# Transposes of probabilities, queries and keys by transposing DMAs, and scores in four PSUM banks, in a two-layer hybrid decoder step

## The chip, the cores and the metric

The kernel runs as one program on one core of a Trainium2 chip. The metric is the time of one execution in device microseconds. Each run executes the whole program once; the times below are of separate runs. The engines are called PE (TensorE matmul), PEld (TensorE weight load), DVE (VectorE), ACT (ScalarE), POOL (GpSimd) and SP (SyncE, which issues all DMAs of this kernel). "Window" means 256 of the 4096 prompt tokens; there are 16 of them.

## The reference

The step has two layers on 4096 prompt tokens and 8 x 4 sample tokens. Layer 0 is a scan plus gated linear attention; the change does not touch it. Layer 1 is sliding-window attention: 16 query heads of 64 on 2 key heads, each block of 128 queries sees its own and the previous block of 128 keys, and a learned sink logit joins the denominator.

```python
def sink_attention(q, k, v, q_pos, k_pos, sinks):
    s = jnp.einsum('...qhgd,...khd->...hgqk', q, k) * (SWA_HEAD_DIM ** -0.5)
    ...
    s = jnp.where(allowed[..., None, None, :, :], s, -jnp.inf)
    sink = sinks.astype(jnp.float32).reshape(SWA_KV_HEADS, SWA_GROUP, 1, 1)
    m = jnp.maximum(jnp.max(s, axis=-1, keepdims=True), sink)
    pr = jnp.exp(s - m)
    denom = jnp.sum(pr, axis=-1, keepdims=True) + jnp.exp(sink - m)
    return jnp.einsum('...hgqk,...khd->...qhgd', pr / denom, v)
...
    q = rope(rms_norm(q.reshape(n, l, SWA_HEADS, SWA_HEAD_DIM), p['q_norm_g']), pos)
    k = rope(rms_norm(k.reshape(n, l, SWA_KV_HEADS, SWA_HEAD_DIM), p['k_norm_g']), pos)
...
    return x + o.astype(x.dtype) @ p['w_out'], ...
```

## The kernel before

The program has three phases; the change lies in `phase2`, layer 1, which takes roughly the last 1400 us. Every float32 matrix product is made of three float16 products (high x high, high x low, low x high), so weights, activations, probabilities, queries and keys exist as pairs of float16 tiles.

For each window, `instream` projects the tokens to q, k, v (`mmA`, lines 334 to 336) and to the gate (`mmB`, lines 325 to 327). `heads` norms and rotates a block of 128 tokens and leaves its high and low halves in `s16`, with tokens in the partitions. `turn` (lines 1565 to 1572) brings the 64-wide heads into the partitions: eight TensorE transposes of 128 x 128 for each half of the queries, four for the keys, into a PSUM tile `pt`, which ACT copies to `qT` or `kT`. For one window that is 2 blocks x (8 + 8 + 4) = 40 transposes.

`attn` goes through 8 units for a window: 2 blocks x 2 groups of 4 heads x 2 key heads. For a unit, `scores` (line 1692) puts 16 matmuls of 128 columns into one PSUM tile of two banks, copies the previous block's half on ACT (line 1703), lays the masked half over it on DVE (line 1706), runs `softmax` (DVE and ACT in turn) and splits the probabilities on ACT (`Ph`, line 1710) and POOL (`Pl`, line 1711). Two units later `turnP` (line 1714) turns both with eight TensorE transposes, ACT copies the result to `PT` (line 1720), and DVE multiplies it by the mask to `PC` (line 1722). `values` then runs the 12 matmuls of two units with `PT` and `PC` (line 1760), and gates the result to `og`. `out` multiplies the `og` of the window before with the output weights (lines 325 to 327), adds the residual (line 1804) and stores it (line 1805).

`merge` interleaves these generators by the costs that they yield and by the weights E1 (attention), E2 (output) and so on. The instructions recorded so are then put in a final order for each engine by the framework's scheduler, which works with estimated times; the engines run that order strictly and meet at semaphores. All DMAs are issued by SP, in one order, and an SP instruction that waits holds all that stand behind it.

The lines that matter for the turns:

```python
                nc.tensor.transpose(pt[:, a, i], s[:, i], self.ident16)
        PT = P.tile([128, 8, 128], F16, name="PT", bufs=2)
        nc.scalar.activation(PT, pt.rearrange("p a i n -> p (a i) n"), AF.Copy, bias=0.0, scale=1.0)
```

Of the kernel before, what the change touches and what calls it, by code (L numbers as in the profile page):

```python
# [36 lines left out]
E1, E2, E3 = 120.0, 70.0, 30.0  # L37
# [69 lines left out]
class K:  # L107
# [1332 lines left out]
    def phase2(self, es1, tail):  # L1440
# [34 lines left out]
        psc = self.pool("p2sc", bufs=1, es=el, space=PSUM)  # L1475
        ppt = self.pool("p2pt", bufs=1, es=el, space=PSUM)
        pmm = self.pmm
        ptt = Rota(self.pta, self.ptb)
        psc = self.pool("p2sc", bufs=1, es=el, space=PSUM)
# [41 lines left out]
        n = NW  # L1521
# [8 lines left out]
        def instream(w):  # L1530
# [22 lines left out]
            for b, t in blocks:  # L1553
# [11 lines left out]
                def turn(i, s16, qT=qT, kT=kT):  # L1565
                    pt = ptt.tile([128, 8, 128], F16, name="pt")
                    for a in range(8 if i < 2 else 4):
                        nc.tensor.transpose(pt[:, a], s16[:, a], self.ident16)  # L1568
                    if i < 2:
                        nc.scalar.activation(qT[:, 8 * i:8 * i + 8], pt, AF.Copy, bias=0.0, scale=1.0)  # L1570
                    else:
                        nc.scalar.activation(kT.rearrange("p a b n -> p (a b) n"), pt[:, 0:4], AF.Copy, bias=0.0, scale=1.0)
# [119 lines left out]
        def scores(W, b, prev, g, kv, out):  # L1692

            ps = psc.tile([128, 4, 2, 128], F32, name="ps")
            for i in range(4):
                q = W["q"][b][:, 2 * (4 * g + i) + kv]
                for a, k in enumerate((prev[0] if prev else None, W["k"][b])):
                    if k is not None:
                        nc.tensor.matmul(ps[:, i, a], q, k[:, kv, 0], start=True, stop=False)  # L1699
                        nc.tensor.matmul(ps[:, i, a], q, k[:, kv, 1], start=False, stop=True)  # L1700
            Sc = P.tile([128, 4, 128], F32, name="Sc", bufs=2)
            if prev:
                nc.scalar.activation(Sc, ps[:, :, 0], AF.Copy, bias=0.0, scale=1.0)
            else:
                nc.gpsimd.memset(Sc, -1e30)
            nc.vector.copy_predicated(Sc, mkc.bitcast(I32)[:, None, :].to_broadcast([128, 4, 128]), ps[:, :, 1])
# [27 lines left out]
        def attn(W, Wp):  # L1734
# [40 lines left out]
            for u in range(11):  # L1775
# [10 lines left out]
                if 2 <= u < 10:  # L1786
                    unit, p = pend.pop(0)
                    pend2.append((unit, turnP(*p)))
                if u < 8:
                    next(sc)  # L1790
                yield 2.8
# [358 lines left out]
```

## Time and profile before

| | us |
|---|---|
| median of 3 runs | 3290.13 |
| lowest and highest | 3287.15, 3292.01 |
| the profiled execution's own time | 3289.11 |
| its span in the trace | 3287.3 |
| PE busy | 3150.1 (96%) |
| DVE, ACT, POOL busy | 2054.4 (62%), 1688.5 (51%), 1261.2 (38%) |

The profile is one execution, taken by the hardware's profiler. A row of instructions gives how long one took and what ended the idle time before it; matmuls overlap each other, so the distance from one to the next, and not the duration of one, is what PE pays for it. The chain is the work that ended last, followed back from the end of the span or of a stretch. The time outside the span is 1.8 us.

### The profile page before, as it was taken

To read this page: it belongs to the slowest core of one execution; us is meant where nothing else is said; L and a number is where in the kernel's file an instruction comes from. 1 tells how busy PE (TensorE), PEld (TensorE's weight loads), DVE (VectorE), ACT (ScalarE), POOL (GpSimd) and SP (SyncE) were. 2 spreads that over 40 slices of the span, in tenths; PEclk is the share of its full clock that TensorE was granted. 3 is DMA by queue.
4 is the path that set the end of the run, shared out by engine and by line. 5 is a ranking of instruction groups with operands and counts; after the bars stand their busy time and mean duration, and the time that the engine had idled before them with its cause. 6 is when DMAs were issued, how large, how long until landed. Compare 5 with 4: busy or idle time off the path is not lost.

```text
span 3287.3 us, 68398 instructions
## 1 busy us (share of the span) xinstructions
PE 3150.1 (96%) x27293; PEld 2458.2 (75%) x27293; DVE 2054.4 (62%) x4785; ACT 1688.5 (51%) x4054; POOL 1261.2 (38%) x1292
## 2 busy tenths in 40 slices
PE   6898879899999999999999999999999999999999
PEld 5687766687788777788877667777777777777777
DVE  8869998644444443444446477666666666666675
ACT  4386556233344343343345366565555656555664
POOL 7824241211111211111111565554555555555552
PEclk9799989999999999999999999999999999999999
DMA  4297467411111112211113212111111111101111
GB/s 128 60 252 176 95 149 223 121 46 49 46 49 46 44 45 71 58 50 46 43 53 122 72 36 62 41 40 41 36 42 40 34 37 37 34 28 41 40 32 43
DMA packets 329521, 222.79 MB, mean 68 GB/s; under 512 B 142544, under 2 KB 302240, under 8 KB 329056
## 3 DMA queue, kind: packets, MB, share of 16 engines
q1 hardware_dynamic: 329200, 218.41, 24.2%
q8 instruction: 214, 3.51, 0.4%
q14 instruction: 107, 0.88, 0.1%
HBM read 164.94 MB, written 53.23 MB: 66 GB/s over the span
## 4 chain that ended last, share of the span: by engine, by line
PE 75%; DVE 11%; ACT 4%; issue 4%; DMA 4%; POOL 3%; SPq 1%; DVEq 0%; POOLq 0%; ACTq 0%
PE mm L325 13%; PE mm L326 13%; PE mm L327 13%; PE mm L334 7%; PE mm L335 7%; PE mm L336 7%; PE po L1760 3%; PE pt L1718 2%; PE ps L1699 2%; PE ps L1700 2%; PE pt L1568 1%; DVE z L777 1%; POOL xl L314 1%; DVE x L312 1%; DMA wst<-in_w_in 1%
## 5 line engine op out<-in xcount | busy, mean ns | idle before, releaser
L325 PE MATMUL mm<-ogh,woh 128*128 128x256 f16 x1472 | 401.3, 273 | 1.4 <-DVE xr L1346 1.4
L326 PE MATMUL mm<-ogl,woh 128*128 128x256 f16 x1472 | 401.3, 273 | 0.5 <-POOL ogl L1772 0.5
L327 PE MATMUL mm<-ogh,wol 128*128 128x256 f16 x1472 | 401.3, 273 | 0.0
L314 POOL TENSOR_TENSOR xl<-x,xh 128x512 f16<-128x512 f32 (+1 forms) x196 | 261.3, 1355 | 319.1 <-ACT xh L313 306.1
L1683 ACT ACTIVATE Sc<-Sc,ng,rq 128x128 f32<-128x128 f32 x512 | 245.6, 482 | 107.1 <-DVE ng L1677 105.7
L272 POOL TENSOR_TENSOR acc<-acc,sq 128x512 f32<-128x512 f32 x48 | 61.8, 1288 | 565.4 <-issue 370.4
L1711 POOL TENSOR_TENSOR Pl<-Sc,Ph 128x512 f16<-128x512 f32 x128 | 153.3, 1198 | 275.6 <-ACT Ph L1710 244.9
L326 PEld LDWEIGHTS <-woh 128*128 128x128 f16 x2112 | 207.2, 98 | 36.4 <-issue 9.8
L325 PEld LDWEIGHTS <-woh 128*128 128x128 f16 x2112 | 207.2, 98 | 31.6 <-issue 4.6
L336 PEld LDWEIGHTS <-xl 128*128 128x128 f16 x1536 | 151.0, 98 | 106.0 <-issue 6.7
L334 PEld LDWEIGHTS <-xh 128*128 128x128 f16 x1536 | 150.9, 98 | 102.5 <-issue 17.7
L327 PEld LDWEIGHTS <-wol 128*128 128x128 f16 x2112 | 207.1, 98 | 25.5 <-issue 3.1
L335 PEld LDWEIGHTS <-xh 128*128 128x128 f16 x1536 | 151.0, 98 | 84.0 <-issue 5.1
L325 PE MATMUL mm<-xh,wuh 128*128 128x256 f16 (+1 forms) x544 | 151.6, 283 | 14.2 <-ACT us L727 6.9
L313 ACT ACTIVATE xh<-x 128x512 f16<-128x512 f32 (+1 forms) x196 | 117.8, 618 | 75.6 <-DVE x L312 61.7
L326 PE MATMUL mm<-xl,wuh 128*128 128x256 f16 (+1 forms) x544 | 151.4, 284 | 4.9 <-POOL xl L314 4.9
L1720 ACT ACTIVATE PT<-pt 128x1024 f16<-128x1024 f16 x128 | 129.6, 1013 | 42.1 <-PE pt L1718 42.1
L327 PE MATMUL mm<-xh,wul 128*128 128x256 f16 (+1 forms) x544 | 151.1, 283 | 0.0
L312 DVE TENSOR_TENSOR x<-x,rb 128x512 f32<-128x512 f32 (+1 forms) x188 | 136.5, 781 | 22.5 <-ACT rb L302 18.2
L1346 DVE SCALAR_TENSOR_TENSOR xr<-mm,soa,xr 128x512 f32<-128x512 f32 x64 | 47.7, 745 | 160.5 <-PE mm L327 155.8
L326 PE MATMUL mm<-xl,wi1gah 128*128 128x256 f16 x512 | 141.4, 277 | 3.0 <-POOL xl L314 3.0
L327 PE MATMUL mm<-xh,wi1gal 128*128 128x256 f16 x512 | 141.0, 276 | 2.4 <-DVE wi1gal L245 2.4
(730 smaller groups left out, 10558.9 us busy)
## 6 DMA issues: line engine op xcount, KB each, us to landing
x<-in_xT SPq DMA_DIRECT2D x128, 256.0 KB
wst<-in_w_in SPq DMA_DIRECT2D x64, 256.0 KB
xr<-in_xT SPq DMA_DIRECT2D x64, 256.0 KB
h_d<-xr SPq DMA_DIRECT2D x64, 256.0 KB
x<-h_d SPq DMA_DIRECT2D x64, 256.0 KB
xr<-h_d SPq DMA_DIRECT2D x64, 256.0 KB
out_yT<-xr SPq DMA_DIRECT2D x64, 256.0 KB
wst<-in_w_out SPq DMA_DIRECT2D x48, 256.0 KB
```

Source lines behind the costliest of these rows:

```text
L312: nc.vector.tensor_mul(x, x, rb[:, None, :].to_broadcast([128, 2, n]))
L313: nc.scalar.activation(h, x, AF.Copy, bias=0.0, scale=1.0)
L314: nc.gpsimd.tensor_sub(l, x, h)
L325: nc.tensor.matmul(ps, wh[:, k0 + k, c], xh[k], start=(k == 0), stop=False)
L326: nc.tensor.matmul(ps, wh[:, k0 + k, c], xl[k], start=False, stop=False)
L327: nc.tensor.matmul(ps, wl[:, k0 + k, c], xh[k], start=False, stop=(k == n - 1))
L334: nc.tensor.matmul(ps, xh[k][:, t], wh[:, k, c0:c1], start=(k == 0), stop=False)
L335: nc.tensor.matmul(ps, xh[k][:, t], wl[:, k, c0:c1], start=False, stop=False)
L336: nc.tensor.matmul(ps, xl[k][:, t], wh[:, k, c0:c1], start=False, stop=(k == n - 1))
L1683: nc.scalar.activation(Sc[:, i], Sc[:, i], AF.Exp, bias=ng[:, i:i + 1], scale=scale[:, i:i + 1], accum_out=de[:, i:i + 1])
L1711: nc.gpsimd.tensor_sub(Pl, Sc, Ph)
L1720: nc.scalar.activation(PT, pt.rearrange("p a i n -> p (a i) n"), AF.Copy, bias=0.0, scale=1.0)
```

## The change

The transposes of `turn` and `turnP` leave TensorE, PSUM and ACT: SP issues a transposing DMA from `s16` to `qT` or `kT`, and from `Pp` (the high and low probabilities, now one tile) to `PT`. The latter is issued as soon as the softmax has ended, into three `PT` buffers where there were two. The multiplication by the mask stays on DVE, in `masked`, called later than `turnP` was. The scores of a unit go in two halves of one bank each, and four banks rotate: two of their own and two that the turns used. The copy on ACT and the masked copy on DVE are made for each half. E2 goes from 70 to 90, and the loop over the units has 10 steps in place of 11.

```diff
-E1, E2, E3 = 120.0, 70.0, 30.0
+E1, E2, E3 = 120.0, 90.0, 30.0
...
-        psc = self.pool("p2sc", bufs=1, es=el, space=PSUM)
+        psc = Rota(self.pool("p2sa", bufs=1, es=el, space=PSUM), self.pool("p2sb", bufs=1, es=el, space=PSUM), self.pta, self.ptb)
...
                 def turn(i, s16, qT=qT, kT=kT):
-                    pt = ptt.tile([128, 8, 128], F16, name="pt")
-                    for a in range(8 if i < 2 else 4):
-                        nc.tensor.transpose(pt[:, a], s16[:, a], self.ident16)
                     if i < 2:
-                        nc.scalar.activation(qT[:, 8 * i:8 * i + 8], pt, AF.Copy, bias=0.0, scale=1.0)
+                        nc.sync.dma_start_transpose(qT[:, 8 * i:8 * i + 8], s16.rearrange("p a n -> p (a n)"))
...
-            ps = psc.tile([128, 4, 2, 128], F32, name="ps")
-            for i in range(4):
...
+            for j in range(2):
+                ps = psc.tile([128, 2, 2, 128], F32, name="pt")
+                for i in range(2):
...
+                So = Sc[:, 2 * j:2 * j + 2]
+                if prev:
+                    nc.scalar.activation(So, ps[:, :, 0], AF.Copy, bias=0.0, scale=1.0)
+                nc.vector.copy_predicated(So, mkc.bitcast(I32)[:, None, :].to_broadcast([128, 2, 128]), ps[:, :, 1])
             yield from softmax(Sc, snk[:, kv, 4 * g:4 * g + 4], W["rq"][b][:, g].rearrange("p (i k) -> p k i", k=2)[:, kv], 2.0**14, P)
-            Ph = P.tile([128, 4, 128], F16, name="Ph", bufs=3)
-            Pl = P.tile([128, 4, 128], F16, name="Pl", bufs=3)
-            nc.scalar.activation(Ph, Sc, AF.Copy, bias=0.0, scale=1.0)
-            nc.gpsimd.tensor_sub(Pl, Sc, Ph)
-            out += [Ph, Pl]
-
-        def turnP(Ph, Pl):
-            pt = ptt.tile([128, 2, 4, 128], F16, name="pt")
-            for a, s in enumerate((Ph, Pl)):
-                for i in range(4):
-                    nc.tensor.transpose(pt[:, a, i], s[:, i], self.ident16)
-            PT = P.tile([128, 8, 128], F16, name="PT", bufs=2)
-            nc.scalar.activation(PT, pt.rearrange("p a i n -> p (a i) n"), AF.Copy, bias=0.0, scale=1.0)
+            Pp = P.tile([128, 2, 4, 128], F16, name="Pp", bufs=2)
+            nc.scalar.activation(Pp[:, 0], Sc, AF.Copy, bias=0.0, scale=1.0)
+            nc.gpsimd.tensor_sub(Pp[:, 1], Sc, Pp[:, 0])
+            PT = P.tile([128, 8, 128], F16, name="PT", bufs=3)
+            nc.sync.dma_start_transpose(PT, Pp.rearrange("p a i n -> p (a i n)"))
+            out.append(PT)
+
+        def masked(PT):
             PC = P.tile([128, 8, 128], F16, name="PC", bufs=2)
             nc.vector.tensor_mul(PC, PT, mT[:, None, :].to_broadcast([128, 8, 128]))
             return PC, PT
...
-            for u in range(11):
+            for u in range(10):
+                if u >= 3 and u % 2:
+                    pend2.append((units[u - 2], masked(*pend.pop(0)[1])))
```

The order of SP in the second half of one window, before: loads of residual tiles (`xr`) and of the rotation table (`rt`), and stores of the output (`out_yT`); what a row waits for stands in brackets, where DMAHW names an earlier DMA's semaphore and the other names an engine.

```order
L1805 DMA out_yT<-xr_29819 128x2x256 [waits DMAHW3_49,DVE_49]
L258 DMA xr_31122<-h1_d_5405 128x2x256 [waits DMAHW4_49,DMAHW3_49]
L1805 DMA out_yT<-xr_29821 128x2x256 [waits DMAHW5_49,DVE_49]
L258 DMA xr_31124<-h1_d_5405 128x2x256 [waits DMAHW6_49,DMAHW5_49]
L1556 DMA rt_31153<-in_rope 128x64 [waits DMAHW7_49,Pool_49]
L1805 DMA out_yT<-xr_29980 128x2x256 [waits DVE_49]
L258 DMA xr_31126<-h1_d_5405 128x2x256 [waits DMAHW1_49,DMAHW0_49]
L1556 DMA rt_31931<-in_rope 128x64 [waits DMAHW7_49,DMAHW2_49,Pool_49]
L258 DMA x_29787<-h1_d_5405 128x2x256 [waits Pool_49]
```

The same stretch of SP in the changed kernel:

```order
L1799 DMA out_yT<-xr_29291 128x2x256 [waits DMAHW6_49,DVE_49]
L258 DMA xr_30362<-h1_d_5405 128x2x256 [waits DMAHW6_49]
L1554 DMA rt_30389<-in_rope 128x64 [waits DMAHW0_49,Pool_49]
L1565 DMA_TRANSPOSE qT_29192<-s16_29860 128x8x128 [waits DMAHW1_49,Pool_49]
L1710 DMA_TRANSPOSE PT_29698<-Pp_29695 128x8x128 [waits PE_49,Pool_49]
L1710 DMA_TRANSPOSE PT_29775<-Pp_29772 128x8x128 [waits DMAHW3_49,PE_49,Pool_49]
L1710 DMA_TRANSPOSE PT_29900<-Pp_29897 128x8x128 [waits DMAHW4_49,DMAHW5_49,PE_49,Pool_49]
L1567 DMA_TRANSPOSE kT_29915<-s16_30146 128x4x128 [waits DVE_49]
L1710 DMA_TRANSPOSE PT_30018<-Pp_30015 128x8x128 [waits DMAHW2_49,PE_49,Pool_49]
L1565 DMA_TRANSPOSE qT_29914<-s16_30200 128x8x128 [waits DMAHW7_49,Pool_49]
L1554 DMA rt_31111<-in_rope 128x64 [waits DMAHW0_49,Pool_49]
L1710 DMA_TRANSPOSE PT_30100<-Pp_30097 128x8x128 [waits DMAHW1_49,DMAHW3_49,PE_49,Pool_49]
```

Fourteen transposing DMAs of a window (8 of `PT`, 4 of `qT`, 2 of `kT`) have come between the loads and stores, and in this stretch they stand close together. Each waits for POOL (or DVE), which writes the last half of its source.

DVE before, around the masked multiplication of two units (line 1722), with the end of a softmax (lines 1686 to 1690) ahead of it:

```order
L1690 TENSOR_TENSOR Sc_29447<-Sc_29447,de_29471 128x512 [waits DVE_49]
L1766 SCALAR_TENSOR_TENSOR og_29514<-po_29501,ga_27617 128x256 [waits PE_49]
L1766 SCALAR_TENSOR_TENSOR og_29514<-po_29501,ga_27796 128x256
L1722 TENSOR_TENSOR PC_29552<-PT_29550,mT_21053 128x1024 [waits Activation_49]
L1599 TENSOR_REDUCE ss_29612<-t2_29611 128x8 [waits Activation_49]
L1600 TENSOR_TENSOR qk_29610<-mm_29528,RC_29323 128x512 [waits PE_49]
```

DVE in the changed kernel, around the same multiplication (now line 1715) of the unit whose `PT` is 29698:

```order
L1704 COPY_PREDICATED Sc_29811<-mkc_21048,pt_29812 128x256 [waits Activation_49]
L1704 COPY_PREDICATED Sc_29811<-mkc_21048,pt_29823 128x256 [waits Activation_49]
L1669 TENSOR_REDUCE mx_29834<-Sc_29811 128x4 [waits DVE_49]
L1715 TENSOR_TENSOR PC_29809<-PT_29698,mT_21050 128x1024 [waits DMAHW2_49]
L1670 TENSOR_TENSOR mx_29834<-mx_29834,rq_28713 128x4 [waits DVE_49]
L1548 SCALAR_TENSOR_TENSOR ga_29783<-ga_29783,mm_29784 128x512 [waits Activation_49]
L1671 TENSOR_TENSOR mx_29834<-mx_29834,snk_21046 128x4 [waits DVE_49]
L1673 TENSOR_SCALAR ng_29838<-mx_29834 128x4 [waits DVE_49]
```

The multiplication now waits for a DMA and no longer for ACT, and it stands inside the softmax of a later unit.

## Rows read from the trace of the kernel before

**Rows 1.** The page: busy time by engine, and granted PE clock in 40 slices.

```profile
PE 3150.1 (96%) x27293; PEld 2458.2 (75%) x27293; DVE 2054.4 (62%) x4785; ACT 1688.5 (51%) x4054; POOL 1261.2 (38%) x1292
PEclk9799989999999999999999999999999999999999
```

**Rows 2.** Stretches: length; busy PE, PEld, DVE, ACT, POOL; clock, DMA share, GB/s.

```profile
2500.00:2600.00 100.00, 100.00 (x929) 76.31 (x928) 60.69 (x142) 56.98 (x142) 53.59 (x63) 1.00 0.11 34
3200.00:3288.00 88.00, 82.66 (x998) 68.62 (x995) 53.20 (x128) 46.06 (x125) 19.00 (x20) 1.00 0.14 40
```

**Rows 3.** The chain of 2400 to 2800 us: shares, then pieces (start, us).

```profile
by line: PE mm L325 16.1%; PE mm L327 16.0%; PE mm L326 16.0%; PE mm L334 10.0%; PE mm L335 9.8%; PE mm L336 9.8%; PE po L1760 7.5%; PE pt L1718 4.0%; PE ps L1700 3.9%; PE ps L1699 3.9%; PE pt L1568 2.9%; PE pt L299 0.3%
...
2457.88 0.45 PE pt L1718 x8
...
2546.35 0.45 PE pt L1718 x8
```

**Rows 4.** PE in a steady window: two matmuls of 256 columns.

```profile
2511.74 0.27 PE L325 MATMUL mm<-ogh,woh 128*128 128x256 f16 x1
2511.85 0.27 PE L326 MATMUL mm<-ogl,woh 128*128 128x256 f16 x1
```

**Rows 5.** Groups by line from 1900 us on: busy us, mean ns, idle before.

```profile
L1720 ACT ACTIVATE PT<-pt 128x1024 f16<-128x1024 f16 x128 | 129.6, 1013 | 42.1 <-PE pt L1718 42.1
L1722 DVE TENSOR_TENSOR PC<-PT,mT 128x1024 f16<-128x1024 f16 x128 | 90.8, 709 | 54.1 <-ACT PT L1720 53.8
L1703 ACT ACTIVATE Sc<-ps 128x512 f32<-128x512 f32 x124 | 73.2, 591 | 16.4 <-PE ps L1700 15.2 <-POOL Pl L1711 0.3
L1570 ACT ACTIVATE qT<-pt 128x1024 f16<-128x1024 f16 x60 | 60.8, 1014 | 40.5 <-PE pt L1568 40.5
L1572 ACT ACTIVATE kT<-pt 128x512 f16<-128x512 f16 x30 | 17.8, 593 | 11.9 <-PE pt L1568 11.9
L302 ACT ACTIVATE rb<-pt 128x256 f32<-128x256 f32 x14 | 5.4, 386 | 0.0
```

**Rows 6.** ACT in one window: the first copy of the scores of three units.

```profile
2561.96 0.58 ACT L1703 ACTIVATE Sc<-ps 128x512 f32<-128x512 f32 x1
...
2574.44 0.59 ACT L1703 ACTIVATE Sc<-ps 128x512 f32<-128x512 f32 x1
...
2620.48 0.60 ACT L1703 ACTIVATE Sc<-ps 128x512 f32<-128x512 f32 x1 [0.45 <-PE ps L1700]
```

**Rows 7.** POOL in the same window: the low probabilities of those units.

```profile
2570.86 1.15 POOL L1711 TENSOR_TENSOR Pl<-Sc,Ph 128x512 f16<-128x512 f32 x1 [7.57 <-ACT Ph L1710]
...
2587.62 1.16 POOL L1711 TENSOR_TENSOR Pl<-Sc,Ph 128x512 f16<-128x512 f32 x1
...
2628.33 1.16 POOL L1711 TENSOR_TENSOR Pl<-Sc,Ph 128x512 f16<-128x512 f32 x1 [2.90 <-ACT Ph L1710]
```

**Rows 8.** SP's issues: a store, and the load that waits for its landing.

```profile
2532.79 0.38 SPq L1805 DMA_DIRECT2D out_yT<-xr  x1
2534.96 0.36 SPq L258 DMA_DIRECT2D xr<-h_d  x1
```

**Rows 9.** SP's waits, 2200 to 3200 us: total us, times, longest.

```profile
SPq L1805 <- DVE xr L1804: 243.9, 43, 10.6
SPq L258 <- DMA out_yT<-xr: 60.2, 32, 3.1
```

**Rows 10.** DMA of 2200 to 3200 us: queue's packets, MB, share of 16 engines.

```profile
q1 hardware_dynamic: 40480, 34.91, 11.6%
...
rt<-in_rope SPq DMA_DIRECT2D x21, 32.0 KB
```

**Rows 11.** The chain from 3180 us to the end.

```profile
by line: ACT Sc L1683 13.5%; PE mm L325 7.7%; PE mm L327 7.6%; PE mm L326 7.5%; issue 6.3%; DVE ng L1677 5.8%; DVE Sc L1706 4.6%; PE po L1760 4.6%; DVE PC L1722 4.3%; DVE mx L1673 4.1%; DVE Sc L1690 4.0%; DVE mx L1675 3.0%; DVE xr L1804 2.5
...
3265.01 1.17 POOL Pl L1711
3268.91 0.77 PE po L1760 x6
```

More of the change, by code (lines that the diff above doesn't have):

```diff
@@ L1474, in phase2 @@
         wo = []
-        psc = self.pool("p2sc", bufs=1, es=el, space=PSUM)
-        ppt = self.pool("p2pt", bufs=1, es=el, space=PSUM)
         pmm = self.pmm
         ptt = Rota(self.pta, self.ptb)
-        psc = self.pool("p2sc", bufs=1, es=el, space=PSUM)
+        psc = Rota(self.pool("p2sa", bufs=1, es=el, space=PSUM), self.pool("p2sb", bufs=1, es=el, space=PSUM), self.pta, self.ptb)
         ppt = self.pool("p2pt", bufs=1, es=el, space=PSUM)
@@ L1565, in turn @@
                 def turn(i, s16, qT=qT, kT=kT):
-                    pt = ptt.tile([128, 8, 128], F16, name="pt")
-                    for a in range(8 if i < 2 else 4):
-                        nc.tensor.transpose(pt[:, a], s16[:, a], self.ident16)
                     if i < 2:
-                        nc.scalar.activation(qT[:, 8 * i:8 * i + 8], pt, AF.Copy, bias=0.0, scale=1.0)
+                        nc.sync.dma_start_transpose(qT[:, 8 * i:8 * i + 8], s16.rearrange("p a n -> p (a n)"))
                     else:
-                        nc.scalar.activation(kT.rearrange("p a b n -> p (a b) n"), pt[:, 0:4], AF.Copy, bias=0.0, scale=1.0)
+                        nc.sync.dma_start_transpose(kT.rearrange("p a b n -> p (a b) n"),
+                                                    s16[:, 0:4].rearrange("p a n -> p (a n)"))
                 for i in (2, 0, 1):
@@ L1692, in scores @@
         def scores(W, b, prev, g, kv, out):
-            ps = psc.tile([128, 4, 2, 128], F32, name="ps")
-            for i in range(4):
[L1696 to L1700, printed above, removed]
@@ L1701, in scores @@
             Sc = P.tile([128, 4, 128], F32, name="Sc", bufs=2)
-            if prev:
-                nc.scalar.activation(Sc, ps[:, :, 0], AF.Copy, bias=0.0, scale=1.0)
-            else:
+            if not prev:
                 nc.gpsimd.memset(Sc, -1e30)
-            nc.vector.copy_predicated(Sc, mkc.bitcast(I32)[:, None, :].to_broadcast([128, 4, 128]), ps[:, :, 1])
-            yield from softmax(Sc, snk[:, kv, 4 * g:4 * g + 4], W["rq"][b][:, g].rearrange("p (i k) -> p k i", k=2)[:, kv], 2.0**14, P)
@@ L1708, in scores @@
-            Ph = P.tile([128, 4, 128], F16, name="Ph", bufs=3)
-            Pl = P.tile([128, 4, 128], F16, name="Pl", bufs=3)
-            nc.scalar.activation(Ph, Sc, AF.Copy, bias=0.0, scale=1.0)
-            nc.gpsimd.tensor_sub(Pl, Sc, Ph)
-            out += [Ph, Pl]
-        def turnP(Ph, Pl):
-            pt = ptt.tile([128, 2, 4, 128], F16, name="pt")
-            for a, s in enumerate((Ph, Pl)):
-                for i in range(4):
-                    nc.tensor.transpose(pt[:, a, i], s[:, i], self.ident16)
-            PT = P.tile([128, 8, 128], F16, name="PT", bufs=2)
-            nc.scalar.activation(PT, pt.rearrange("p a i n -> p (a i) n"), AF.Copy, bias=0.0, scale=1.0)
+            for j in range(2):
+                ps = psc.tile([128, 2, 2, 128], F32, name="pt")
+                for i in range(2):
+                    q = W["q"][b][:, 2 * (4 * g + 2 * j + i) + kv]
+                    for a, k in enumerate((prev[0] if prev else None, W["k"][b])):
+                        if k is not None:
+                            nc.tensor.matmul(ps[:, i, a], q, k[:, kv, 0], start=True, stop=False)
+                            nc.tensor.matmul(ps[:, i, a], q, k[:, kv, 1], start=False, stop=True)
+                So = Sc[:, 2 * j:2 * j + 2]
+                if prev:
+                    nc.scalar.activation(So, ps[:, :, 0], AF.Copy, bias=0.0, scale=1.0)
+                nc.vector.copy_predicated(So, mkc.bitcast(I32)[:, None, :].to_broadcast([128, 2, 128]), ps[:, :, 1])
@@ L1785, in attn @@
                     yield 2.8
-                if 2 <= u < 10:
-                    unit, p = pend.pop(0)
-                    pend2.append((unit, turnP(*p)))
                 if u < 8:
                     next(sc)
+                if u >= 2 and u % 2 == 0:
+                    pend2.append((units[u - 2], masked(*pend.pop(0)[1])))
                 yield 2.8
```

## The prediction

> **What bounds the kernel now.** I read the page first. PE is busy 96% of the span and at full clock nearly everywhere; no other engine passes 62% [rows 1]. A busy PE may still be one that waits, so I looked at stretches of phase 2: in 2500 to 2600 us PE is busy all 100 us, DVE 61, ACT 57, POOL 54 [rows 2]. Then the chain of 2400 to 2800 us: it never leaves PE. The same group of eight transposes returns after 88.47 us (2457.88, 2546.35), which is the length of a window, and it takes 0.45 us, so a transpose costs PE 56 ns. The transposes of the probabilities hold 4.0% of this chain and those of queries and keys 2.9% [rows 3]. The steady windows are bound by what PE has to issue. The last window is not: its chain goes through ACT and DVE [rows 11], and PE has gaps [rows 2].
>
> **The change part by part.**
>
> *PE loses the transposes.* 8 units x 8 + 40 = 104 a window, by 56 ns = 5.85 us; by the chain's shares 6.9% of 88.47 = 6.1 us [rows 3]. I take 5.85. While `attn` works on one of the first 15 windows, PE is the bound: 15 x 5.85 = 88 us. In the last one I count nothing.
>
> *ACT and DVE.* ACT loses 128 copies of 1.013 us, 64 of 1.014 and 32 of 0.593 = 214 us. Halving the score copy costs it 2 x 386 - 591 = 181 ns for each of 128 units, 23 us [rows 5]; the masked copy on DVE should lose something similar, some 20 us. Neither is on the path: a window leaves DVE a third of its time free and ACT more [rows 2]. The cover of both is PE's work. Four banks in rotation free PE of nothing, since it did not wait for the two.
>
> *The transposing DMA itself.* The trace has none, so its price T (issue to landing, for 128 x 1024 float16, 256 KB) is bounded. The low end is a plain 256 KB store: the load that waits for it issues 2.17 us after it (2532.79 to 2534.96) [rows 8]. For the other end the trace gives a price for each packet: 11.6% of 16 engines for 1000 us over 40480 packets is 45.9 ns [rows 10]. Number by number, 131072 packets would hold the 16 engines for 376 us; that is the far end. A turned tile is a set of 1024 rows of 128 numbers, 256 bytes, the size of a row of the rotation table (32 KB over 128 partitions) [rows 10]: 1024 x 45.9 / 16 = 2.9 us on the engines, and with the fixed part of the plain store (2.17 less 256 packets of 1 KB, 0.73 us, so 1.44) T = 4.4 us. I take this one, as rows of 256 bytes are the nearest thing that the trace shows.
>
> *Does 4.4 us fit?* In the changed order a unit's last score matmul and its first value matmul have PE work between them. For the tightest unit (`PT` 29698) that is 108 matmuls of 256 columns, which start 0.11 us apart [rows 4], 43 of 128 columns (56 ns) and 13 value matmuls (0.77 us for six [rows 11]): 11.9 + 2.4 + 1.7 = 16.0 us. Others of the window have 17 to 25, two of the first block up to 37; queries and keys have at least 23. What must fit in: from the first score copy on ACT to the end of `Pl` on POOL it is 10.05 us in one unit (2561.96 to 2572.01), 9.0 in the shortest of a window and 14.3 in the longest [rows 6, 7]; then T, and the multiplication, 0.7 [rows 5]. 10.05 + 4.4 + 0.7 = 15.2 us: it just fits. A long one, 14.3 + 5.1 = 19.4, is some 2 us late in a place that has 17. I count 1 us in half of the 16 windows: +8 us.
>
> *Queues.* A window gets 8 + 4 + 2/2 = 13 whole transposes. At 2.9 us they hold the DMA engines for 38 us of 82.6, beside the 11.6% there now. In the dense stretch of SP's order seven and a half of them fall into some 33 us of PE work, which allows 4.4 us for each: it passes at 2.9. On DVE the multiplication now waits for a DMA, and behind it stands the rest of the next unit's softmax; whatever is late there delays that unit too. The loads of `x` and `xr` behind a waiting transpose were fetched early and their waits cost nothing now, as the chain shows none of them [rows 3].
>
> *The end.* The last unit's turn (0.45 us on PE, 1.01 on ACT) becomes 4.4 us, between `Pl` and the value matmuls, which are on the chain [rows 11]: +3 us.
>
> **Sum.** The profiled execution took 3289.1 us (span 3287.3 and 1.8 around it), 1.0 below the median of the runs shown. 3289.1 - 88 + 8 + 3 = 3212 us; as a median 3213. I say 3212, 2.4% less.
>
> Two rules speak to T, and they disagree. The Trainium skill, "VectorE: DVE Perf Modes", section "The three transpose paths", gives 390 ns for a 128 x 128 transpose on TensorE and 1309 ns by the DMA crossbar. The trace does not agree with the first in this setting: a transpose in a row of eight costs 56 ns. By the second, eight blocks one after another would be an estimated 10.5 us for a tile, 136 us for a window, and the time some 4050 us or more. The Trainium skill, "Advanced Engine Details and Errata", section "X-Bar Transpose (TRN2)", says that such DMAs are as fast as regular ones; by that T is near 2.2 us, nothing is late, and the sum is 3202 us. No run so far shows which holds.
>
> **Rivals.**
>
> A. *The queue of transposes becomes the bound, and the kernel slower.* Place: SP and the DMA engines, in the steady windows. It decides from 88.47 us less 9.5 for 13 plain transfers (0.73 each), by 13: from 6.1 us for each transpose no gain is left. That is a cut into pieces a little over twice as fine as 256 bytes, at 45.9 ns a piece. Pieces of 64 bytes: 11.8 us each, 153 + 9.5 = 162 us for a window, 3289 + 16 x 74 = 4470 us. At 8 us: 113 us a window, 3690. For it: nothing in the trace shows a DMA that turns, and its pieces can only be finer than those of a copy. Against it: DMA is 11% busy [rows 2].
>
> B. *T between 4.6 and 6 us.* The tight units come late. With T = 6 the typical unit is 1.1 us late, the dense stretch runs 7.5 x (6 - 4.4) = 12 us behind if each holds the queue for all of T and not at all if they overlap. Half of that, 6 us a window, eats the gain: 3289 - 88 + 90 = 3291; a quarter, 3246. I say 3230 to 3290.
>
> C. *SP's order holds the transposes.* SP waits 5.7 us at a store for DVE (243.9 by 43), and 1.9 us at the load behind it [rows 9]; before, nothing urgent stood behind them, now transposes do. If one tight unit of a window comes 5.2 us late by this, 15 x 5.2 = 78 us are lost: 3282; with two, 3360. Against it: SP's rows are in the order in which they are expected to come ready, and the densest transposes stand in a row behind the last store.
>
> **How the numbers follow.** A measurement of this kernel tells 0.2%, 6.6 us, from no change. Forecast (T up to 4.6 us, 3195 to 3230): 0.56. B: 0.16, two thirds of it faster by more than that bound. A: 0.20, all slower but a sliver. C: 0.08, half slower, the rest near no change. Faster: 0.56 + 0.10 = 0.66; slower: 0.19 + 0.04 + 0.03 from B = 0.26; same 0.08. The range starts at 3190, where T is that of a plain copy and ACT's relief helps the last window too, and goes to 3400, which takes in B and C and the shallow end of A; it leaves out A's rest, some 0.17. The likeliest case alone has 3195 to 3230.
>
> **What would show it.** Right: the rows of transposes gone from PE and 214 us of copies from ACT; a window of 82 to 84 us between equal places of the chain; transposing DMAs that land 2 to 5 us after issue; PE still busy all of 2500 to 2600; PE waiting for the multiplication by the mask for less than 1 us a window. Wrong: DVE idle before that multiplication for microseconds and the chain passing through it or through DMA; SP's issues of transposes several us apart; a window of 88 us or more; PE's granted clock falling below 1.00 in the steady windows, which would mean that it has gaps.

## The result, and the profile after

| | before | after |
|---|---|---|
| median, us | 3291.07 (4 runs, 3287.15 to 3293.09) | 3242.89 (4 runs, 3238.67 to 3246.22) |
| profiled execution's own time, us | 3289.11 | 3246.22 |
| span, us | 3287.3 | 3244.4 |

The ratio is 0.9854 with the interval 0.9837 to 0.9871: faster by 1.5%, 48 us, where 2.4% and some 79 us were forecast. The page's busy times, which answer to [rows 1]:

```profile
PE 3076.1 (95%) x25629; PEld 2375.9 (73%) x25629; DVE 2028.6 (63%) x4913; ACT 1505.5 (46%) x3954; POOL 1272.1 (39%) x1292
```

PE has 1664 matmuls fewer, ACT 183 us less busy time, where 214 - 23 = 191 were worked out. Two windows of the steady and of the last stretch, beside [rows 2]:

```profile
2500.00:2600.00 100.00, 98.84 (x824) 73.09 (x822) 66.71 (x169) 46.62 (x149) 56.07 (x66) 1.00 0.35 86
3200.00:3244.00 44.00, 38.90 (x526) 33.08 (x524) 20.54 (x51) 12.07 (x43) 9.21 (x11) 1.00 0.41 103
```

PE is no longer busy all of the hundred, though its clock stays at 1.00. What it waits for stands in the waits of 2200 to 3100 (engine and instruction, what came last, us in total, times, longest); PE had none before.

```profile
PE po L1753 <- DMA PT<-Pp: 17.7, 14, 2.8
```

```profile
DVE PC L1715 <- DMA PT<-Pp: 110.0, 50, 7.5
DVE de L1682 <- ACT sn L1680: 68.8, 59, 2.2
```

Both engines wait for turned probabilities: PE at the value matmuls, DVE at the multiplication by the mask.

**Where the 43 us of the two spans lie.** The first key projection of a window is a mark on PE that both kernels have. These are its rows in the fourth and in the last window (duration, first and last start in the piece of time asked for), and the last state update of phase 1, of the kernel before:

```profile
L1121 PE MATMUL pt<-v,kT x256: 272/323/472, 524.1 to 1796.4; 128*64 128x128 f32 x128
L334 PE MATMUL mm<-wi2kvh,xh x5: 272/272/273, 2068.5 to 2071.5; 128*128 128x256 f16 x5
L334 PE MATMUL mm<-wi2kvh,xh x4: 272/272/273, 3135.0 to 3137.7; 128*128 128x256 f16 x4
```

and of the changed kernel:

```profile
L1121 PE MATMUL pt<-v,kT x256: 272/323/477, 529.2 to 1803.0; 128*64 128x128 f32 x128
L334 PE MATMUL mm<-wi2kvh,xh x3: 272/273/273, 2069.4 to 2071.1; 128*128 128x256 f16 x3
L334 PE MATMUL mm<-wi2kvh,xh x5: 272/273/273, 3096.6 to 3099.5; 128*128 128x256 f16 x5
```

| part of the span | forecast | measured, us |
|---|---|---|
| to the end of phase 1 | 0 | 1796.4 to 1803.0: +6.6 |
| first three windows, to the mark | 3 x (-5.85 + 0.5) = -16 | 272.1 to 266.4: -5.7 |
| twelve windows between the marks | 12 x (-5.85 + 0.5) = -64 | 1066.5 to 1027.2: -39.3 |
| from the last mark to the end | +3.5 | 152.3 to 147.8: -4.5 |
| sum | -77 | -42.9 |

Phase 1 is the same code; over the profiled executions of all kernels its end lies between 1796.3 and 1809.2 with no relation to the edit, so those 6.6 us are not the change's. The steady windows are what has to be explained: 88.9 us before, 85.6 after, 83.5 by the forecast, 83.05 if the transposes had simply gone.

The twelve windows can be taken apart on PE. Each matmul gets the distance from its start to the next start, less the idle time that the profile records there (over 0.15 us); the sums between the two marks are, in us, with those of `e7_no_wait`, a run described below, beside them:

| PE, twelve windows | before | after | e7_no_wait |
|---|---|---|---|
| turns, and a few other transposes | 75.4 | 2.6 | 2.6 |
| projections, in and out | 825.0 | 824.7 | 821.0 |
| score matmuls | 86.9 | 96.3 | 89.1 |
| value matmuls | 79.2 | 83.9 | 68.1 |
| recorded waits | 0 | 19.7 | 0.2 |
| sum | 1066.5 | 1027.2 | 981.0 |

So the turns gave back 72.7 us, where 12 x 5.85 = 70.2 were expected, and 34 us of it were lost again: 19.7 in waits and 14 in score and value matmuls that start further apart.

**The place.** One unit, from its scores to its value matmuls, in the changed kernel (start, us, engine, line, and in brackets the idle time before it and what ended that):

```profile
2559.55 0.63 ACT L1703 ACTIVATE Sc<-pt 128x256 f32<-128x256 f32 x2
2562.07 0.69 DVE L1715 TENSOR_TENSOR PC<-PT,mT 128x1024 f16<-128x1024 f16 x1 [0.24 <-DMA PT<-Pp]
2565.40 0.17 DVE L1673 TENSOR_SCALAR ng<-mx 128x4 f32<-128x4 f32 x1
2565.60 0.49 ACT L1679 ACTIVATE Sc<-Sc,ng,rq 128x128 f32<-128x128 f32 x1 [3.46 <-DVE ng L1673]
2566.94 0.91 DVE L1715 TENSOR_TENSOR PC<-PT,mT 128x1024 f16<-128x1024 f16 x1 [1.17 <-DMA PT<-Pp]
2570.64 0.69 DVE L1686 TENSOR_TENSOR Sc<-Sc,de 128x512 f32<-128x512 f32 x1
2571.42 0.63 ACT L1707 ACTIVATE Pp<-Sc 128x512 f16<-128x512 f32 x1 [2.18 <-issue]
2572.38 1.16 POOL L1708 TENSOR_TENSOR Pp<-Sc,Pp 128x512 f16<-128x512 f32 x1
2573.57 1.23 SPq L1710 DMA_TRANSPOSE PT<-Pp  x1
2575.16 0.27 PE L325 MATMUL mm<-xh,wi2g1h 128*128 128x256 f16 x1
2576.67 0.69 DVE L1715 TENSOR_TENSOR PC<-PT,mT 128x1024 f16<-128x1024 f16 x1 [2.89 <-DMA PT<-Pp]
2576.69 0.81 PE L1753 MATMUL po<-PT,vv 128*64 128x512 f16 x5 [1.04 <-DMA PT<-Pp]
```

From the first score copy to the end of the split: 14.0 us (2559.55 to 2573.54); two other units' mask multiplications and their waits stand on DVE within it. SP issues 0.03 us later. The transpose lands 3.10 us after that (2573.57 to 2576.67). PE has come to the value matmuls 16 us after the score copy and stands still: from the matmul at 2575.16 to the next start are 1.53 us in place of 0.11. This is the last unit of a window. In the next window the last unit (scores copied on ACT from 2643.76) is late in another way:

```profile
2656.12 0.63 ACT L1707 ACTIVATE Pp<-Sc 128x512 f16<-128x512 f32 x1 [1.89 <-issue]
2657.44 1.66 POOL L1602 TENSOR_TENSOR rs<-ss,mhalf 128x8 f32<-128x8 f32 x1
2659.07 1.25 POOL L1633 TENSOR_TENSOR qk<-qk,t 128x512 f32<-128x512 f32 x1
2660.70 1.15 POOL L1708 TENSOR_TENSOR Pp<-Sc,Pp 128x512 f16<-128x512 f32 x1
2665.18 0.69 DVE L1715 TENSOR_TENSOR PC<-PT,mT 128x1024 f16<-128x1024 f16 x1 [7.13 <-DMA PT<-Pp]
2665.20 0.81 PE L1753 MATMUL po<-PT,vv 128*64 128x512 f16 x5 [1.39 <-DMA PT<-Pp]
```

ACT has the high half at 2656.75, but POOL does the next heads' work first and ends the low half at 2661.85: 18.1 us from the score copy. The two forms alternate, and in each of the eleven windows that end between 2200 and 3100 PE waits at its last unit, 0.4 to 2.8 us, 15.2 of the 17.7 us.

### The profile page after: what moved, and what is told of

The parts are those of the page before. It is cut to its first block, busy times and chain, and to the rows that moved or that the text cites. A ratio compares the mean times of both kernels' runs of the same rounds, so it can differ in the third digit from the quotient of the medians.

```text
span 3244.4 us, 65819 instructions
## 1 busy us (share of the span) xinstructions
PE 3076.1 (95%) x25629; PEld 2375.9 (73%) x25629; DVE 2028.6 (63%) x4913; ACT 1505.5 (46%) x3954; POOL 1272.1 (39%) x1292
## 5 line engine op out<-in xcount | busy, mean ns | idle before, releaser
L1679 ACT ACTIVATE Sc<-Sc,ng,rq 128x128 f32<-128x128 f32 x512 | 245.8, 482 | 153.0 <-DVE ng L1673 152.3
L326 PEld LDWEIGHTS <-woh 128*128 128x128 f16 x2112 | 207.4, 98 | 41.8 <-issue 13.1
L1708 POOL TENSOR_TENSOR Pp<-Sc,Pp 128x512 f16<-128x512 f32 x128 | 153.0, 1197 | 209.8 <-ACT Pp L1707 202.0
L1715 DVE TENSOR_TENSOR PC<-PT,mT 128x1024 f16<-128x1024 f16 x128 | 98.1, 766 | 154.3 <-DMA PT<-Pp 151.0
L312 DVE TENSOR_TENSOR x<-x,rb 128x512 f32<-128x512 f32 (+1 forms) x188 | 138.8, 791 | 18.7 <-ACT rb L302 11.5
```

Of the source, the lines that this page charges most:

```text
L312: nc.vector.tensor_mul(x, x, rb[:, None, :].to_broadcast([128, 2, n]))
L326: nc.tensor.matmul(ps, wh[:, k0 + k, c], xl[k], start=False, stop=False)
L1679: nc.scalar.activation(Sc[:, i], Sc[:, i], AF.Exp, bias=ng[:, i:i + 1], scale=scale[:, i:i + 1], accum_out=de[:, i:i + 1])
L1708: nc.gpsimd.tensor_sub(Pp[:, 1], Sc, Pp[:, 0])
```

## The experiments

In the table, "twelve windows" is the distance between the same two marks, read as above. Each ratio is to runs of before on the same chip, whose medians were 3291.1 to 3295.1.

| run | time, us | ratio to before | twelve windows, us |
|---|---|---|---|
| before | 3291.07 | 1 | 1066.5 |
| the changed kernel | 3242.89 | 0.9854 [0.9837, 0.9871] | 1027.2 |
| e1_qk_dma | 3260.20 | 0.9889 [0.9873, 0.9905] | 1037.1 |
| e2_p_dma | 3284.66 | 0.9969 [0.9958, 0.9979] | 1053.4 |
| e3_halves_pe | 3299.67 | 1.0018 [1.0006, 1.0029] | 1068.7 |
| e4_values_free | 3234.95 | 0.9816 [0.9798, 0.9834] | 1016.3 |
| e12_mask_free | 3237.94 | 0.9834 [0.9818, 0.9851] | 1017.9 |
| e7_no_wait | 3224.19 | 0.9797 [0.9775, 0.9820] | 981.0 |
| e5_twice | 3321.75 | 1.0081 [1.0052, 1.0110] | 1084.6 |
| e6_apart | 3256.35 | 0.9893 [0.9874, 0.9913] | 1041.0 |
| e8_order | 3238.61 | 0.9844 [0.9824, 0.9864] | 1023.4 |
| e8b_first | 3241.11 | 0.9849 [0.9829, 0.9870] | 1027.1 |
| e9_carry | 3296.77 | 1.0010 [0.9999, 1.0021] | 1078.9 |
| e10_last_pe | 3238.78 | 0.9835 [0.9820, 0.9850] | 1018.9 |

### The parts alone

`e1_qk_dma`: before, with queries and keys turned by DMA and nothing else.

```diff
-                        nc.tensor.transpose(pt[:, a], s16[:, a], self.ident16)
...
-                        nc.scalar.activation(qT[:, 8 * i:8 * i + 8], pt, AF.Copy, bias=0.0, scale=1.0)
+                        nc.sync.dma_start_transpose(qT[:, 8 * i:8 * i + 8], s16.rearrange("p a n -> p (a n)"))
```

> The kernel before with only the turns of queries and keys by transposing DMA; probabilities stay on TensorE. Theory L (the 30 us missing from the forecast are units whose transposed probabilities land late; the transposes of queries and keys have over 23 us of room): PE loses 40 transposes a window at 56 ns, 2.24 us, and nothing is late: 15.5 x 2.24 = 35 us, about 3256 us, a window of 86.2 us. Rival M (the transposing traffic itself slows PE or the other engines, by 3.1 us a window for 13 whole transposes): 5 of 13 of that loss stays, 1.2 us a window, about 3274 us.

`e2_p_dma`: the changed kernel with `turn` as it was, so that only the probabilities go by DMA.

```diff
-                        nc.sync.dma_start_transpose(qT[:, 8 * i:8 * i + 8], s16.rearrange("p a n -> p (a n)"))
+                        nc.scalar.activation(qT[:, 8 * i:8 * i + 8], pt, AF.Copy, bias=0.0, scale=1.0)
```

> The changed kernel with the turns of queries and keys back on TensorE and ACT; probabilities by DMA. Theory L: PE gains back 2.24 us of work a window, but this work also stands between scores and values and gives the late units room, so some of the lateness goes: 3250 to 3278 us, a window of 86 to 88 us. Rival M: 8 of 13 of 3.1 us a window stay, 3291 - 54 + 29 = 3266 us, with PE hardly waiting at the value matmuls.

`e3_halves_pe`: before with the scores in halves, in two banks in rotation, and E2 = 90; all turns on TensorE.

```diff
-E1, E2, E3 = 120.0, 70.0, 30.0
+E1, E2, E3 = 120.0, 90.0, 30.0
...
-            ps = psc.tile([128, 4, 2, 128], F32, name="ps")
+            for j in range(2):
+                ps = psc.tile([128, 2, 2, 128], F32, name="pt")
```

> No transposing DMA at all: the kernel before with the scores in halves of one bank (two banks in rotation) and E2 = 90. Theory L: PE's work is that of before and nothing is late, 3285 to 3297 us. Rival H (the halves on ACT and DVE or the new weight E2 cost the missing time): 3.1 us a window more, about 3335 us.

The halves and E2 cost 5 us, 2 to 10 by the interval, and 2.2 of it in the twelve windows. Queries and keys give 29.4 us in twelve windows, where 12 x 40 x 56 ns = 26.9 were expected. The probabilities, with the halves and E2, give 13.1 where 12 x 64 x 56 ns = 43.0 were expected. The two gains add up to that of the whole change (42.5 against 39.3), so what is missing is missing at the probabilities: 30 us in twelve windows, 2.5 a window. By their ratios `e1_qk_dma` takes 3255 us, as L had it, and `e2_p_dma` 3281, a little past L's range.

### Who waits

`e4_values_free`: the value matmuls read a fixed tile, so that only DVE waits.

```diff
-                                         pend2[kv][1][p2][:, 4 * lo:4 * lo + 4].rearrange("p i n -> p (i n)"),
+                                         W2["g0"][0][:, 2 * p2 + lo, 0:512],
```

> The changed kernel, but the value matmuls read a fixed tile of weights in place of PT and PC, so that PE waits for no transposed probability; all transposing DMAs and the multiplication by the mask on DVE still run, and the attention output is wrong. Theory L: PE is bound by its work alone, a window of 82.6 us, 3291 - 91 = about 3200 us. Rival M: the traffic is all there, so the window stays near 85.7 us, about 3243 us. If DVE, held by the mask multiplication, is late for other consumers of PE as well, something between, 3215 us.

Only 11 us came back in the twelve windows, and the whole, some 3230 us by the ratio, fits none of the three forecasts. Nor do the 11 us come from less waiting: the value matmuls now stand in undivided groups of twelve and take 68.1 us between the marks, 15.8 less than in the changed kernel, while PE's recorded waits are 24 us there in place of 20. In 2200 to 3100 they are now others:

```profile
PE mm L336 <- POOL xl L314: 11.3, 14, 1.3
PE po L1753 <- DVE og L1759: 7.6, 7, 1.6
```

Both inputs come by way of DVE (the scaling of `x` before `xl`, and `og`), which still stands at the mask multiplication.

`e12_mask_free`: the other way round, the mask multiplication reads a fixed tile and PE waits.

```diff
-            nc.vector.tensor_mul(PC, PT, mT[:, None, :].to_broadcast([128, 8, 128]))
+            nc.vector.tensor_mul(PC, W2["g0"][0][:, 0:2, 0:512].rearrange("p a (i n) -> p (a i) n", n=128), mT...)
```

> The changed kernel with the mask multiplication reading a fixed weight tile, so that DVE never stands behind a transpose, while the value matmuls still read the turned probabilities and PE waits for them (it leaves out the product of turned probabilities and mask). It is the fourth of a set: both wait (the changed kernel, 3243), only DVE waits (3235), neither waits (3224). If DVE's standing is what lengthens the next unit's softmax and makes the turns late (H1): as good as with no wait at all, 3222 to 3230. If PE's own wait for the transfer is the cost and DVE only shares it (H2): near the changed kernel, 3238 to 3244.

```profile
PE po L1753 <- DMA PT<-Pp: 19.7, 12, 2.1
```

9 us came back, and H1 falls: with DVE free of the turns, PE waits for the transfer as long as before (21 us between the marks, against 20).

`e7_no_wait`: both edits.

> The changed kernel with all its transposing DMAs issued as they are, but the multiplication by the mask and the value matmuls read a fixed weight tile of the same shape, so that neither DVE nor PE waits for a transpose of probabilities (it leaves out the use of the turned probabilities, so the attention output is not the reference's). Theory H (the 30 us that are missing come from engines that stand in order behind a transpose that has not landed: DVE at the multiplication by the mask, 110 us in 900, and PE at the value matmuls): the forecast without its late waits, about 3206 us, at most 3215. Rival M (the transposing DMAs slow the work by their traffic or by holding SP, whoever waits): 3228 us or more, no better than the 3235 of the run in which PE alone did not wait.

PE waits for nothing from 2200 to 3100 and is busy throughout:

```profile
2500.00:2600.00 100.00, 100.00 (x878) 77.07 (x876) 64.45 (x158) 49.28 (x151) 57.55 (x69) 1.00 0.39 92
```

Its marks, in the fourth and the last window:

```profile
L334 PE MATMUL mm<-wi2kvh,xh x4: 272/273/273, 2098.1 to 2100.7; 128*128 128x256 f16 x4
L334 PE MATMUL mm<-wi2kvh,xh x4: 272/272/273, 3079.1 to 3081.7; 128*128 128x256 f16 x4
```

The twelve windows take 981.0 us, 46 less than in the changed kernel, with the same transposing DMAs (DMA share 0.39 against 0.35). So in the steady windows M is refuted: with the same traffic and the same issues on SP, PE is held up nowhere once no engine waits for a turn. The whole time came down by only 19 us, and so missed H's number, because this kernel reaches the fourth window 28.7 us later (2098.1 against 2069.4): with nothing to wait for, the scheduler put the first attention units early (the first from 1854.5 us, against 1889.0), and DVE was full there (50.00 of 50 us from 1950 to 2000, PE 41.73). Not all 46 us are the waits' either. By the table of PE's time, 19.5 us are recorded waits that have gone. Another 15.8 are the value matmuls: freed of their inputs they stand in 48 undivided groups of twelve, where the changed kernel has 117 pieces and the kernel before 96. The score matmuls give 7.2 and the projections 3.7. So this run prices the recorded waits at some 20 us, and what is missing beyond them lies in the order on PE; why the scheduler divides the groups so was not tried.

One wait alone taken away brought 9 or 11 us, and PE still waited 21 or 24 us between the marks; with both taken away it waits 0.2. PE and DVE wait for the same landing, and the wait that is left holds PE in place of the one that went.

### The size of T

`e5_twice`: a second, equal transpose into the same tile behind the first.

```diff
             nc.sync.dma_start_transpose(PT, Pp.rearrange("p a i n -> p (a i n)"))
+            nc.sync.dma_start_transpose(PT, Pp.rearrange("p a i n -> p (a i n)"))
```

> The changed kernel with each transpose of probabilities issued twice in a row into the same tile, so that what the engines wait for lands later by one transposing DMA, 0.7 us (two that follow each other landed 3.75 us after issue, one alone 3.1) to 3.1 us, and nothing else differs. Theory H: PE's wait at the last pair of each window grows by the whole of that, and a second pair of the window comes late too: 1 to 6 us a window, 3258 to 3335 us. Rival M (the waits cost little, traffic is what costs): the DMA engines' share rises from 3 to 5 tenths and the time by twice what it now costs, the same in all stretches, with PE's waits for the turn unchanged near 18 us in 900.

75 us more than the changed kernel by the ratios, 4.8 in each of the twelve windows, and the waits for the turn grow threefold:

```profile
PE po L1754 <- DMA PT<-Pp: 53.2, 24, 4.7
```

H holds: there is no room left in which a longer T could hide. The delay is at the upper end of what was expected: SP issues the second transpose 3.1 us behind the first (the median), so what the engines wait for lands about 7 us after the first issue. Not all of the 57 us in the twelve windows is waiting. PE's recorded waits there are 45 us more; the granted clock was 0.98 over 2200 to 3100, against 1.00 in the changed kernel, and the projections take 11 us more (835 in place of 824.7).

`e6_apart`: the high half turned right behind ACT's copy, the low half behind POOL's subtraction.

```diff
-            nc.sync.dma_start_transpose(PT, Pp.rearrange("p a i n -> p (a i n)"))
+            nc.sync.dma_start_transpose(PT[:, 0:4], Pp[:, 0].rearrange("p i n -> p (i n)"))
+            nc.gpsimd.tensor_sub(Pp[:, 1], Sc, Pp[:, 0])
+            nc.sync.dma_start_transpose(PT[:, 4:8], Pp[:, 1].rearrange("p i n -> p (i n)"))
```

> The changed kernel with the transpose of a unit cut in two: the high half is issued behind ACT's copy, the low half behind POOL's subtraction, 64 KB and half the columns each. If the wait is for the transfer itself, the smaller last piece lands 0.5 to 1 us sooner and the time falls by 5 to 12 us, 3231 to 3238. If each transpose mainly holds SP or has a fixed time of its own (the keys' half-size one held SP 1.19 us, the full one 1.23), twice as many make it worse: 3250 or more.

13 us worse, the second case. A half holds SP as long as a whole, and in SP's queue the low half here stands behind a transpose of queries that took its turn first:

```profile
2571.89 1.19 SPq L1709 DMA_TRANSPOSE PT<-Pp  x1
2573.12 1.33 SPq L1565 DMA_TRANSPOSE qT<-s  x1
2574.49 1.26 SPq L1711 DMA_TRANSPOSE PT<-Pp  x1
```

It lands at 2577.12, 2.63 us after its issue, where the whole one took 3.10: half the size saves 0.5 us.

### Attempts to take the wait away

`e8_order` and `e8b_first` move only the order (`issue_after` puts what is recorded in the block behind the named instruction on its engine):

```diff
-                    pend2.append((units[u - 2], masked(*pend.pop(0)[1])))
+                    with behind(mks[u - 1], "de"):
+                        pend2.append((units[u - 2], masked(*pend.pop(0)[1])))
```

and, in `e8_order` alone, the same with "ng" for the second unit and "s" for `values()`.

> The changed kernel with another order on two engines and nothing else: on DVE the mask multiplication of a pair's first unit is issued behind the second unit's last softmax product, that of the second unit behind the maximum of the unit after it; on PE the value matmuls behind the scores of that unit. Theory H: DVE's waits at the multiplication fall from 110 us in 900 to under 50, PE's from 18 to under 10, and half or more of the missing 30 us come back: 3215 to 3230 us. Rival M: no better than the changed kernel, 3240 or more.

> Only the first of the three: the mask multiplication of a pair's first unit behind the second unit's last softmax product. Theory H: these multiplications are wanted only with the second one's, so DVE waited for nothing at them; its waits go from 110 us in 900 to about 60, and the next unit's softmax comes earlier by that: 3230 to 3238 us. Rival M: 3243, no change.

Both missed: by the ratio 3 and 2 us better than the changed kernel, and inside its interval. DVE still waits 106.8 us in 900 in both, against 110.0, and 67.9 of it, where it was 53.6, at one unit of each window, as here in `e8_order`:

```profile
2570.40 0.69 DVE L1548 SCALAR_TENSOR_TENSOR ga<-ga,mm 128x512 f32<-128x512 f32 x1 [0.72 <-ACT ga L1547]
2577.72 0.69 DVE L1718 TENSOR_TENSOR PC<-PT,mT 128x1024 f16<-128x1024 f16 x1 [6.64 <-DMA PT<-Pp]
```

It is the window's last unit again: no later unit of the window is there behind which it could be put. At the other seven units DVE's waits fell from some 57 to 39 us without a gain that is clear of noise; PE's own waits stayed (19.2 us, against 17.7). Since the total hardly fell, these two runs don't price DVE's waits.

`e9_carry`: the last unit's values go behind the next window's first scores.

```diff
+                if u == 9 and W is not Ws[-1]:
+                    held.append(rest)
+                    break
...
+                    if u == 0 and held:
+                        held.pop()()
+                        yield 2.8
...
+            yield lambda: W["vals"] == 4
             yield from outstream(W, n * w)
```

> The changed kernel with one thing moved: the second mask multiplication and the value matmuls of a window's last pair of units are recorded behind the scores of the next window's first unit, and the output projection of that window waits for them. In the changed kernel PE waits 1.0 to 2.9 us at just this place in each of the ten windows of 2200 to 3100, while at the other three pairs it waits little; by the program's order the work between the last unit's scores and its value matmuls grows from 17.3 to 22 us. Theory H (the missing time is PE's wait for a late turn, the same place in every window): 1.2 to 1.6 us less in each of 15 windows, 3218 to 3228 us. If the waits only move to the next pair, or the output projection that now starts later opens a gap of its own: 3238 to 3248.

Wrong by far, past the rival's number too: 51 us worse than the changed kernel by the ratios. PE waits 38.2 us in 900, 20 times, and 28 of it still at the same unit, 2.7 to 2.9 us in each window:

```profile
2583.51 0.77 DVE L1704 COPY_PREDICATED Sc<-mkc,pt 128x256 f32<-128x256 int32 x2
2602.17 1.44 PE L1755 MATMUL po<-PT,vv 128*64 128x512 f16 x5 [2.83 <-DMA PT<-Pp]
```

Its values come 18.7 us after its scores, but the scores had moved later as well, and the place that was to have 22 us has 16 without the wait. What is queued behind these values (`og`, and now the whole output projection) starts later by as much. Between the marks PE's recorded waits are 51.5 us in place of 19.7, which explains 32 of the 52 us that the twelve windows lost. The rest is at the projections, 844 us in place of 824.7, and the clock shows there. Behind the wait shown the granted clock was 0.50, the lower of its two levels (1.2 GHz), and then 1.00 again (the last numbers but two of these rows); matmuls of 256 columns start 0.21 us apart in the first stretch and 0.11 in the second:

```profile
2602.00:2605.00 3.00, 2.83 (x13) 1.44 (x13) 2.85 (x6) 0.00 (x0) 2.62 (x2) 0.50 0.47 122
2606.00:2609.00 3.00, 3.00 (x20) 1.44 (x18) 1.86 (x8) 0.91 (x2) 0.25 (x1) 1.00 0.28 83
```

Over 2200 to 3100 the granted clock is 0.98 here and 1.00 in the changed kernel.

`e10_last_pe`: the last of the eight units is turned on TensorE, as before the change; seven by DMA.

```diff
+                if u == 8:
+                    pend[1][1][0] = turnP(pend[1][1][0])
```

> The changed kernel with one of the eight units of a window, the last, turned as before: eight transposes on TensorE into one of the four rotating banks and a copy on ACT, asked for one step before its values; the other seven by DMA. This is the unit at whose value matmuls PE waited 1.0 to 2.9 us in each window of 2200 to 3100. Theory H: PE pays 8 x 56 ns = 0.45 us and no longer waits there, 0.8 to 1.2 us a window, 3224 to 3232 us. If the wait moves to another pair, as it did when this pair's values were put later, or the order changes elsewhere: 3243 or more.

8 us better in the twelve windows, 0.7 each where 0.8 to 1.2 were expected. The waits at this unit's value matmuls are gone, and DVE's at the multiplication fall from 110 to 54 us:

```profile
PE po L1764 <- DMA PT<-Pp: 3.3, 6, 1.6
PE pt L1719 <- ACT Pp L1707: 2.2, 3, 0.9
```

```profile
DVE PC L1726 <- DMA PT<-Pp: 36.0, 37, 2.4
DVE PC L1726 <- ACT PT L1721: 17.9, 10, 4.0
```

So the place is right, and its price can be read: between the marks PE's recorded waits are 14 us less than in the changed kernel, and its transposes take 5.5 us more. The whole, 3238.78 us, is above H's range, and with `e8_order`'s 3238.61 the lowest of the kernels that compute everything, but its interval overlaps that of the changed kernel: no version here is shown to beat it. Not tried: the split on POOL ahead of the next heads' work, which the second form of the wait suggests.

## Why the prediction was right in sign and 30 us off

*PE loses the transposes.* Right. The steady stretch is bound by what PE issues, the queries' and keys' part came in full (29.4 us against 26.9), and without waits PE is busy throughout (`e7_no_wait`).

*Late long units, +8 us.* This is the step that failed, by its size. The text had the case: a long one of 14.3 us plus T and the multiplication is "some 2 us late in a place that has 17". The last unit of a window is just that one: 14.0 us of softmax and 3.1 of transfer with PE there after 16, or 18.1 and 3.3 with PE there after 20. It was counted as 1 us in half the windows. But the engines run the same order in each window, so a long softmax doesn't fall on a tight place by chance: here it does so every time. The trace of before had this too: from the first score copy to the end of `Pl` its last unit takes 14.3 us in ten of the twelve windows (the fourth to the fifteenth), and no other unit over 12 but in the fifteenth. In the changed kernel it got longer still, in every second window, by POOL's other work. PE's recorded waits are 1.7 us a window (17.7 x 85.6 / 900), where 0.5 was counted: some 14 us more in twelve windows.

*The order on PE, +0.* The windows are 2.5 us longer than without the transposes (85.6 against 83.05), so the waits are not the whole of it. Another 14 us in twelve windows are the score and value matmuls that start further apart (96.3 and 83.9 us, in place of 86.9 and 79.2), which the sum put at nothing; the turns themselves gave 2.5 us more than it said. The value matmuls stand in 117 pieces and come directly behind score matmuls 69 times, where it was 96 pieces and 11 times. `e3_halves_pe`, with the halves and no transposing DMA, has the score matmuls at 86.9 us and the value matmuls at 81.5, and `e2_p_dma` at 93.3 and 84.9, so it comes with the probabilities' DMA for the most part; by what step is open. The part on queues had also said, without a price, that DVE stands at the multiplication with the next unit's softmax behind it; that price was not measured alone.

*Three windows counted as steady that are not.* In the first three windows PE is not the bound all the time; from 1900 to 2000 it is busy 96.4 us before and 92.5 after. They gave 5.7 us of some 16. Rows of that stretch were to be had beforehand, and the sum of 15 equal windows went past them.

*T.* 4.4 us taken, 3.1 measured in most of the transposes of probabilities for which DVE waited, up to 5.1 in a few. The number of pieces was right: the DMA queue of 2200 to 3200, beside [rows 10],

```profile
q1 hardware_dynamic: 203216, 75.43, 33.6%
```

has 162736 packets more, which is 13930 in a window of 85.6 us and 1072 for each of 13 transposes (1024 rows of 256 bytes were assumed). Their price was not: (33.6 - 11.6)% of 16 x 1000 us over 162736 is 21.6 ns, not 45.9, so a tile holds the engines 1.4 us and not 2.9. A T that was too long hid the other error in part: with 3.1 in its place, and the lateness still counted by halves, the sum would have been further off.

By the Trainium skill, "VectorE: DVE Perf Modes", section "The three transpose paths", eight blocks would have taken an estimated 10.5 us; the trace has 3.1. By the Trainium skill, "Advanced Engine Details and Errata", section "X-Bar Transpose (TRN2)", they are as fast as regular DMAs; the trace has 3.1 against 2.17 for the plain store of [rows 8], 0.9 us longer and so nearer to this page than to the other.

*ACT and DVE.* The masked copy in halves costs DVE 2 x 437 ns in place of 728, 19 us in all where some 20 were said. `e3_halves_pe` puts all of the halves and E2 at 5 us where nothing was charged.

*The end.* +3 us were said, and two transposes do stand on its chain (start, us):

```profile
3200.39 3.44 DMA PT<-Pp
3212.83 3.38 DMA PT<-Pp
```

But from the last mark on the kernel is 4.5 us shorter, not longer. The profiles of the parts have 149.8 us there in `e1_qk_dma`, 155.1 in `e2_p_dma` and 154.9 in `e3_halves_pe`, against 152.3 before. As far as one execution of each tells, the queries and keys shorten it, the halves and E2 lengthen it, and the probabilities' DMA adds 0.2 to these and not 3; the parts alone don't add up to the 4.5.

*Rivals.* A did not come: 1.4 us on the engines for each transpose is far from 6.1. C did not come either: in all 96 transposes of probabilities of the twelve windows SP issued within 0.1 us of the end of the split. In B's working the typical unit at T = 6 is 10.05 + 6 + 0.7 = 16.8 us against 16.0, so 0.8 us late and not 1.1; nothing else rests on it. The time fell into B's band (3230 to 3290) and out of the likeliest's own (3195 to 3230), but not by B's cause: T was shorter than forecast, and the softmax ahead of it was the long part.

*The signs named beforehand.* They came out mixed: the window of 85.6 us lies between "82 to 84" and "88 or more", PE is 98.84 us busy in 2500 to 2600 and not all of it, the clock there stays at 1.00, and DVE's idle time before the multiplication, of up to 7.5 us, is the sign of being wrong that came.

## What to carry to other kernels

When a schedule repeats, a coincidence of a long chain with a tight place happens in every period or in none: compare the two unit by unit and charge the lateness in full, not by a share. When several in-order engines wait for the same transfer, taking one wait away shows little, since the other holds the same work; take all of them away in one run, and read the waits themselves in it, since the edit also changes the order. A transfer that replaces work on the bound engine is worth only what the slack between its source and its first reader covers.

## What was not expected of the hardware

A transposing DMA of 128 x 1024 float16 between tiles of SBUF held SP for 1.23 us and landed 3.1 us after its issue; half the size held SP 1.19 to 1.26 us and landed after 2.6. A plain DMA issue held it 0.35 us (the load of the rotation table). The price of a packet of 256 bytes was 21.6 ns in the transposes, less than half of the mean of the plain transfers of this kernel (45.9).

A wait of PE can cost more than its length: behind one of 2.83 us in `e9_carry` the granted clock was 0.50 for some 3 us, and over 2200 to 3100 it was 0.98 in that run and in `e5_twice`, against 1.00 in the changed kernel.
